# The first norm of a decoder block on one core: rows scaled in place and transposed plainly, the first tokens' products in unsplit fp32, and an earlier place for some weight loads

## The chip, the cores and the metric

One core of a Trainium2 chip runs the whole kernel. The metric is the device time of one launch in microseconds (us); the median of several runs is compared with the median of the kernel before. PE is the matmul engine (TensorE), DVE the vector engine, ACT the scalar engine, POOL is GpSimd, and SP is the engine that issues most loads.

## The reference

```python
# x (512 tokens, 2048), w_in (2048, 3*1024 + 3*1024 + 8 + 2*2048)
h = rmsnorm(x, g_mix)                       # x * rsqrt(mean(x*x) + 1e-6) * g_mix
z = einsum('bsd,dc->bsc', h, w_in)          # all input projections at once
cb, cc, cv, q, k, v, f_logit, gate_c, gate_a = split(z)
conv_y = cb * causal_dwconv(cc * cv, conv_w)
attn = forgetting_attention(q, k, v, log_sigmoid(f_logit + b_f))
merged = sigmoid(gate_c + b1) * (conv_y @ w_conv_out) + sigmoid(gate_a + b2) * (attn @ w_attn_out)
x = x + merged @ w_mix_out
x = x + square(relu(rmsnorm(x, g_mlp) @ w_ff1)) @ w_ff2
out = rmsnorm(x, g_final)
```

All of it is float32. The change lies in the first norm and in the first products with `w_in`.

## The kernel before

**Number format.** A matmul in plain fp32 is avoided in the products. Each operand is cut into a high part, rounded to the reduced format fp32r (`high_of`, ACT, line 111), and the rest, the low part (`low_of`, DVE, line 114). A product is then three matmuls: high by high, low by high, and high by low.

**Tiling.** The 512 tokens are four row tiles of 128 (`xin[0]` to `xin[3]`, 128x2048 each, 1 MB). The 2048 channels are 16 chunks of 128; chunks are taken in pairs, of which the even ones are "parity 0" and the odd ones "parity 1". The products follow a Strassen-like scheme on halves of the tokens and of the channels. For a group of columns the names are A11 and A12 (first half of the tokens, even or odd chunks), A22 (second half of the tokens, odd chunks), and S1 to S4 (sums of halves). `Q1.H[i, par]` holds the normed and transposed tokens of token half i and parity par in fp32; `Q1.ST["A11"]` and so on hold their high and low parts. A group (`Group`) loads its weights in four quarters, `X[i, j]`, 128 x 8 x 256 floats each (1 MB), into four slots. `head` computes the A11 and A12 products, `tail2` the rest. The first group is `gV0`; `heads[1]` is `keys`, the first pair of key and query heads; `heads[2]` to `heads[4]` follow.

**The stage that the change touches** is the first 40 us. Instructions that are `tied` stay in the order in which the program gives them on their engine (`strict[0]`); the others are placed by a scheduler. The order of the kernel before is this:

- SP loads row tile 0 (two halves), `gV0.X[0, 0]` (two pieces), row tile 1 (two halves), `gV0.X[1, 0]`, row tiles 2 and 3, and then the keys' two quarters.
- PE first runs 11 dummy matmuls (`stay_awake`) and transposes the norm's gains (`pv`, line 742).
- ACT and DVE sum the squares of row tile 0 in three pieces. POOL raises the mean to the power -0.5 (`factor`, line 716). DVE multiplies the identity by this factor (line 751, `dgs[0]`), and `Q1.turn` (line 592) multiplies each chunk of rows with this scaled identity, which transposes and scales it at once, in plain fp32. `Q1.gained` (line 600, DVE) takes it out of PSUM and multiplies by the gains.
- `block` (line 697) does the products of one row tile with one weight quarter, kind 0 (high by high), 1 (low rows) and 2 (low weights): 24 matmuls of 256 columns. Tile 0 with A11, then tile 0 with A12, tile 1 with A11, tile 1 with A12, with the turning of tile 1 in between.
- Row tiles 2 and 3 are scaled in place (line 805 on ACT, line 806 on DVE), and `turn_both` and `gained_both` (lines 608, 616, 618) transpose them by plain transposes, 32 in number, through four PSUM banks; DVE takes out four of the eight pairs of chunks and ACT the other four.
- The keys' weights are split (lines 111 and 114), gV0's two sums are added, and A22 is split. Then `g.head()` runs for `heads[1]` and the following groups (`mm_cols`, lines 171, 175 and 177: 48 matmuls of 256 columns a product), then `Q1.sums()`, then the tails, gV0's first (lines 195 to 199).

The high and low parts of weights lie in buffers `th` and `tl`, two of each (`places`).

Of the kernel before, what the change touches and what calls it, by code (L numbers as in the profile page):

```python
# [8 lines left out]
F32 = mybir.dt.float32  # L9
# [36 lines left out]
def tile_hybrid_block(ctx: ExitStack, tc, x, g_mix, w_in, b_f, b_gate, conv_w, w_conv_out,  # L46
# [509 lines left out]
    class Quarters:  # L556
# [134 lines left out]
    def block(n, ps, t, hi, lo, kinds, qs=range(KT // 2)):  # L691

        o, ts = ps[:, t * VW:(t + 1) * VW], slice(t * P, (t + 1) * P)
        for kind in kinds:
            for q in qs:
                Sh, Sl = (e[:, ts] for e in Q1.moving(n)(q))
                tied(nc.tensor.matmul(o, Sl if kind == 1 else Sh, (lo if kind == 2 else hi)[:, q, :],
                                      start=t == 0 and kind == 0 and q == 0, stop=kind == 2 and q == KT // 2 - 1,
                                      skip_group_check=True))

# [23 lines left out]
    nc.vector.memset(ss1[:, :, 4:], EPS)  # L724
    strict[0] = True
    load_rows(0, 2, (nc.sync,))
    gains, rows = both[:KT, 0, S:S + P], both[:NV - KT, 0, S + P:S + 2 * P]
# [28 lines left out]
    tied(nc.gpsimd.dma_start(out=rows[r0:r0 + 3 * CT, :], in_=conv_w[0].rearrange("j (k p) -> (j k) p", p=P)))
    tied(nc.vector.tensor_copy(cols[:, :KT], pv[:, :KT]))
    even, odd = Q1.turn(0, 0, (0, 1)), Q1.turn(0, 1, (2, 5))
    stay_awake(1)
    early, late = range(KT // 4), range(KT // 4, KT // 2)  # L760
    hi1, lo1 = gV0.places()
    for qs in (slice(0, KT // 4), slice(KT // 4, KT // 2)):
        high_of(gV0.X[0, 0][:, qs], hi1[:, qs])
    for n in range(2):
        Q1.gained(0, 0, n, even[n])
    A11, A12 = (Q1.cut(n, 0) for n in ("A11", "A12"))
    high_of(*A11[:2])
    squares(1, 1)
    Q1.gained(0, 1, 0, odd[0])
    low_of(*A11)  # L770
    low_part(gV0.X[0, 0], hi1, lo1, early)
    v = mean_of(1)
    Q1.gained(0, 1, 1, odd[1])
    tied(nc.scalar.activation(out=dgs[1], in_=ident, func=AF.Copy, scale=factor(v)))
    high_of(*A12[:2])
    low_part(gV0.X[0, 0], hi1, lo1, late)
    a, b = (gV0.acc(k)[0] for k in "ab")
    block("A11", a, 0, hi1, lo1, (0, 1))
    block("A11", a, 0, hi1, lo1, (2,), early)
    even = Q1.turn(1, 0, (6, 7))  # L780
    block("A11", a, 0, hi1, lo1, (2,), late)
    odd = Q1.turn(1, 1, (0, 1))
    pv = bank(2, "pv")
    tied(nc.tensor.transpose(pv[:, :NV - KT], rows, ident[:NV - KT, :NV - KT]))
    hi2, lo2 = gV0.places()
    high_of(gV0.X[1, 0], hi2)
    for n in range(2):
        Q1.gained(1, 0, n, even[n])
    low_of(*A12)
    block("A12", b, 0, hi2, lo2, (0, 1))  # L790
    A11, A12 = (Q1.cut(n, 1) for n in ("A11", "A12"))
    high_of(*A11[:2])
    low_of(*A11)
    squares(2, 1)
    squares(3, 1)
    for n in range(2):
        Q1.gained(1, 1, n, odd[n])
    r2 = factor(mean_of(2))
    low_part(gV0.X[1, 0], hi2, lo2, early)
    low_part(gV0.X[1, 0], hi2, lo2, late)  # L800
    r3 = factor(mean_of(3))
    high_of(*A12[:2])
    low_of(*A12)
    tied(nc.scalar.activation(out=cols[:, KT:], in_=pv[:, :NV - KT], func=AF.Copy))
    tied(nc.scalar.activation(out=xin[2], in_=xin[2], func=AF.Copy, scale=r2))
    tied(nc.vector.tensor_scalar(out=xin[3], in0=xin[3], scalar1=r3, scalar2=None, op0=ALU.mult))
    block("A11", a, 1, hi1, lo1, (0, 1, 2))
    block("A12", b, 0, hi2, lo2, (2,))
    block("A12", b, 1, hi2, lo2, (0, 1, 2))
    tied(nc.gpsimd.dma_start(out=bf, in_=b_f.to_broadcast([P, NH])))  # L810
    gV0.a, b = [a], [b]
    keys.ready["A11"] = hi3, lo3 = keys.places()
    high_of(keys.X[0, 0], hi3)
    Q1.tiles("A22")
# [1138 lines left out]
```

## Time and profile before

| | |
|---|---|
| median of 3 runs | 2400.08 us (2398.72 to 2400.45) |
| the profiled execution | 2399.19 us, span of the core 2397.5 us, mean granted clock 0.999 |
| PE busy | 2381.4 us, 99% of the span |
| DVE busy | 2039.6 us, 85% |
| ACT busy | 1235.8 us, 52% |
| POOL busy | 283.0 us, 12% |
| the chain that ended last | PE 91%, DVE 4%, issue 2%, ACT 2%, DMA 1% |

The span is the time from the first to the last instruction of one profiled execution. The run's own time is 1.7 us longer. A plain fp32 matmul leaves two records on PE, the other matmuls leave one.

### The profile page before, as it was taken

To read this page: it belongs to the slowest core of one execution; us is meant where nothing else is said; L and a number is where in the kernel's file an instruction comes from. 1 tells how busy PE (TensorE), PEld (TensorE's weight loads), DVE (VectorE), ACT (ScalarE), POOL (GpSimd) and SP (SyncE) were. 2 spreads that over 40 slices of the span, in tenths; PEclk is the share of its full clock that TensorE was granted. 3 is DMA by queue.
4 is the path that set the end of the run, shared out by engine and by line. 5 is a ranking of instruction groups with operands and counts; after the bars stand their busy time and mean duration, and the time that the engine had idled before them with its cause. 6 is when DMAs were issued, how large, how long until landed. Compare 5 with 4: busy or idle time off the path is not lost.

```text
span 2397.5 us, 41341 instructions
## 1 busy us (share of the span) xinstructions
PE 2381.4 (99%) x17742; PEld 2253.0 (94%) x17742; DVE 2039.6 (85%) x1684; ACT 1235.8 (52%) x1301; POOL 283.0 (12%) x451
## 2 busy tenths in 40 slices
PE   9999999999999999999999999999999999999998
PEld 9999999999999999899999999999998888888886
DVE  8987787888888778889988989888897888889898
ACT  7443656445545534356666666666664333333334
POOL 1100111121111202012200000000001001100000
PEclk9999999999999999999999999999999999999999
DMA  8665544555465756476856465565688557665662
GB/s 279 184 191 154 172 145 151 169 193 173 159 215 175 265 178 223 147 221 223 322 196 232 169 229 198 198 228 198 231 296 302 166 186 254 220 221 183 228 235 98
DMA packets 282199, 491.98 MB, mean 205 GB/s; under 512 B 11676, under 2 KB 191992, under 8 KB 281632
## 3 DMA queue, kind: packets, MB, share of 16 engines
q1 hardware_dynamic: 229280, 277.96, 36.4%
q0 software_dynamic: 49968, 206.39, 23.5%
q10 hardware_dynamic: 2768, 4.99, 0.6%
q8 instruction: 139, 2.28, 0.4%
q14 instruction: 44, 0.36, 0.0%
HBM read 379.70 MB, written 109.07 MB: 204 GB/s over the span
## 4 chain that ended last, share of the span: by engine, by line
PE 91%; DVE 4%; issue 2%; ACT 2%; DMA 1%; POOL 0%; DVEq 0%; POOLq 0%; ACTq 0%; SPq 0%
PE a L171 6%; PE a L175 6%; PE a L177 6%; PE a L199 5%; PE a L195 5%; PE a L197 5%; PE d L171 5%; PE d L175 5%; PE d L177 5%; PE c L177 4%; PE c L171 4%; PE c L175 4%; PE d L197 3%; PE d L195 3%; PE d L199 3%; PE b L171 3%
## 5 line engine op out<-in xcount | busy, mean ns | idle before, releaser
L111 ACT ACTIVATE th<-x 128x2048 fp32r<-128x2048 f32 (+2 forms) x281 | 537.2, 1912 | 454.5 <-DVE x L128 163.0
L114 DVE TENSOR_TENSOR tl<-x,th 128x2048 fp32r<-128x2048 f32 (+2 forms) x282 | 638.9, 2271 | 149.9 <-ACT th L111 144.1
L128 DVE TENSOR_TENSOR x<-x,x 128x2048 f32<-128x2048 f32 (+1 forms) x160 | 365.5, 2285 | 22.1 <-DMA x<-in_w_in_dram 19.4
L111 ACT ACTIVATE th<-y 128x2048 fp32r<-128x2048 f32 (+1 forms) x109 | 185.4, 1702 | 273.4 <-PE a L197 138.7
L114 DVE TENSOR_TENSOR tl<-y,th 128x2048 fp32r<-128x2048 f32 (+1 forms) x109 | 219.2, 2012 | 25.0 <-ACT th L111 24.5
L195 PE MATMUL a<-th,us 128*128 128x512 f32 x508 | 197.7, 389 | 0.0
L197 PE MATMUL a<-th,us 128*128 128x512 f32 x508 | 197.6, 389 | 0.0
L171 PE MATMUL c<-S,th 128*128 128x256 f32 x848 | 195.4, 276 | 0.0
L175 PE MATMUL c<-S,th 128*128 128x256 f32 x848 | 195.1, 276 | 0.0
L171 PE MATMUL a<-S,th 128*128 128x256 f32 x784 | 180.9, 277 | 0.0
L175 PE MATMUL a<-S,th 128*128 128x256 f32 x784 | 180.2, 276 | 0.0
L171 PEld LDWEIGHTS c<-S,th 128*128 128x128 f32 x848 | 159.2, 188 | 0.0
L175 PEld LDWEIGHTS c<-S,th 128*128 128x128 f32 x848 | 159.2, 188 | 0.0
L175 PEld LDWEIGHTS a<-S,th 128*128 128x128 f32 x784 | 147.3, 188 | 0.0
L171 PEld LDWEIGHTS a<-S,th 128*128 128x128 f32 x784 | 147.2, 188 | 0.0
L199 PE MATMUL a<-tl,us 128*128 128x512 f32 x508 | 135.7, 389 | 0.0
L171 PE MATMUL a<-A,th 128*128 128x256 f32 x544 | 125.7, 277 | 0.0
L171 PE MATMUL b<-A,th 128*128 128x256 f32 x544 | 125.5, 276 | 0.0
L171 PE MATMUL d<-S,th 128*128 128x256 f32 x544 | 125.5, 277 | 0.0
L175 PE MATMUL b<-A,th 128*128 128x256 f32 x544 | 125.4, 276 | 0.0
L175 PE MATMUL a<-A,th 128*128 128x256 f32 x544 | 125.4, 276 | 0.0
L171 PE MATMUL d<-A,th 128*128 128x256 f32 x544 | 125.3, 276 | 0.0
(428 smaller groups left out, 6056.9 us busy)
## 6 DMA issues: line engine op xcount, KB each, us to landing
x<-in_w_in_dram SPq DMA_DIRECT2D x85, 1024.0 KB, 5.7
y<-in_w_ff_dram SPq DMA_DIRECT2D x64, 1024.0 KB, 7.4
x<-in_w_ff_dram SPq DMA_DIRECT2D x60, 1024.0 KB, 8.4
us<-s_d POOLq DMA_DIRECT2D x44, 1024.0 KB, 9.0
s_d<-rh POOLq DMA_DIRECT2D x32, 896.0 KB, 5.7
s_d<-r POOLq DMA_DIRECT2D x32, 896.0 KB, 5.8
x<-in_w_mix_out_dram SPq DMA_DIRECT2D x17, 1024.0 KB, 6.7
g_d<-o POOLq DMA_DIRECT2D x32, 256.0 KB, 3.2
```

What stands on the lines that cost most here:

```text
L111: return tied(nc.scalar.activation(out=hi, in_=src, func=AF.Copy))
L114: return tied(nc.vector.tensor_tensor(out=lo, in0=src, in1=hi.bitcast(F32), op=ALU.subtract))
L128: return nc.vector.tensor_tensor(out=out, in0=a, in1=b, op=ALU.subtract)
L171: i = nc.tensor.matmul(o, hi[:, q, js], Sh, start=first and q == 0 and j == 0, stop=False, skip_group_check=True)
L175: nc.tensor.matmul(o, hi[:, q, js], Sl, start=False, stop=False, skip_group_check=True)
L177: i = nc.tensor.matmul(o, lo[:, q, js], Sh, start=False, stop=q == nq - 1, skip_group_check=True)
L195: tied(nc.tensor.matmul(o, Sh, hi[:, q, :], start=begin and q == 0, stop=False, skip_group_check=True))
L197: tied(nc.tensor.matmul(o, Sl, hi[:, q, :], start=False, stop=False, skip_group_check=True))
L199: tied(nc.tensor.matmul(o, Sh, lo[:, q, :], start=False, stop=q == nq - 1, skip_group_check=True))
```

## The change

Row tiles 0 and 1 are scaled in place, the even chunks by DVE and the odd ones by ACT (`scaled`), and are turned by plain transposes. The products of row tile 0 with both weight quarters, and those of row tile 1 with the first half of the first quarter, are made in plain fp32 from `Q1.H` and the loaded weights (`whole_block`); the other products of row tile 1 stay split (`part_block`). For the split ones only the second half of the first weight quarter is cut (`pieces`), in buffers of their own. The squares of row tile 1 are also taken in three pieces; as written, the pieces of row tile 1 begin at columns 0, 512 and 1536, those of row tile 0 at columns 0, 1024 and 1536. The gains are copied out of PSUM by DVE before the last piece of the squares of row tile 0. `gV0.X[1, 0]` is loaded before row tile 1, and the keys' two quarters before row tiles 2 and 3. Row tile 2 is scaled by DVE, not by ACT. The keys' two weight quarters are split within the tied order, and the turning of row tiles 2 and 3 goes between the two products of the keys' head (`between=rest_turned`), with the split of A22 behind it.

```diff
-                    tied(nc.tensor.matmul(pt[:, k, :], xin[t][:, c * P:(c + 1) * P], dgs[t], start=True, stop=True))
+                    tied(nc.tensor.transpose(pt[:, k, :], xin[t][:, c * P:(c + 1) * P], ident))
...
-    dgs = [both[:, 0, t * P:(t + 1) * P] for t in range(2)]
+    early, late = range(KT // 4), range(KT // 4, KT // 2)
+    front, back = slice(0, KT // 4), slice(KT // 4, KT // 2)
...
+    def scaled(t, par, qs, r, vector=True):
+
+        o = xin[t].rearrange("p (q two c) -> p two q c", two=2, c=P)[:, par, qs]
+        if vector:
+            tied(nc.vector.tensor_scalar(out=o, in0=o, scalar1=r, scalar2=None, op0=ALU.mult))
+        else:
+            tied(nc.scalar.activation(out=o, in_=o, func=AF.Copy, scale=r))
+
+    def whole_block(par, ps, t, X, qs):
+
+        o, ts = ps[:, t * VW:(t + 1) * VW], slice(t * P, (t + 1) * P)
+        for q in qs:
+            tied(nc.tensor.matmul(o, Q1.H[0, par][:, q, ts], X[:, q, :], start=t == 0 and q == 0, stop=False,
+                                  skip_group_check=True))
...
+    gV0.ahead(1, 0)
     load_rows(1, 2, (nc.sync,))
-    gV0.ahead(1, 0)
-    load_rows(2, 1, (nc.sync,))
-    load_rows(3, 1, (nc.sync,))
     keys = heads[1]
     keys.ahead(0, 0)
     keys.ahead(1, 0)
+    load_rows(2, 1, (nc.sync,))
+    load_rows(3, 1, (nc.sync,))
     awake, pv = bank(3, "awake"), bank(7, "pv")
     stay_awake(11)
     tied(nc.tensor.transpose(pv[:, :KT], gains, ident[:KT, :KT]))
-    stay_awake(2)
...
+    stay_awake(4)
+
+    squares_by_scalar(0, 0, 0, 1024)
+    squares_by_scalar(0, 1, 1024, 512)
+    tied(nc.vector.tensor_copy(cols[:, :KT], pv[:, :KT]))
+    squares_by_vector(0, 2, 1536, 512)
+    r0 = factor(sum_of(0))
...
+    scaled(0, 0, front, r0)
+    scaled(0, 1, slice(0, KT // 2), r0, False)
+    scaled(0, 0, back, r0)
     even, odd = Q1.turn(0, 0, (0, 1)), Q1.turn(0, 1, (2, 5))
...
+    whole_block(0, a, 0, first, range(KT // 2))
+    for n in range(2):
+        Q1.gained(0, 1, n, odd[n])
+    pieces = [(first[:, q:q + 2], otile([P, 2, VW], "wh", F32R), otile([P, 2, VW], "wl", F32R)) for q in late[::2]]
+    for x2, h2, l2 in pieces:
+        high_of(x2, h2)
...
+    whole_block(1, b, 0, second, range(KT // 2))
+    hi2, lo2 = gV0.places()
+    high_of(second[:, front], hi2[:, front])
+    squares_by_scalar(1, 0, 0, 1024)
+    squares_by_scalar(1, 1, 512, 512)
+    for piece in pieces:
+        low_of(*piece)
+    squares_by_vector(1, 2, 1536, 512)
+    r1 = factor(sum_of(1))
+    high_of(second[:, back], hi2[:, back])
+    low_part(second, hi2, lo2, early)
+    scaled(1, 0, slice(0, KT // 2), r1)
+    scaled(1, 1, slice(0, KT // 2), r1, False)
+    even, odd = Q1.turn(1, 0, (6, 7)), Q1.turn(1, 1, (0, 1))
...
+    keys.ready["A11"] = hi3, lo3 = keys.places()
+    high_of(keys.X[0, 0], hi3)
...
+    whole_block(0, a, 1, first, early)
...
+    part_block("A11", a, of_first, (0, 2, 1), late)
+    part_block("A12", b, of_second, (0, 2), range(KT // 2))
+    low_of(*A12)
+    part_block("A12", b, of_second, (1,), range(KT // 2))
+    low_of(*A11a)
+    low_of(keys.X[0, 0], hi3, lo3)
+    A12 = Q1.cut("A12", 0)
+    high_of(*A12[:2])
...
     squares(2, 1)
     squares(3, 1)
+    keys.ready["A12"] = hi4, lo4 = keys.places()
+    high_of(keys.X[1, 0], hi4)
     r2 = factor(mean_of(2))
+    tied(nc.vector.tensor_scalar(out=xin[2], in0=xin[2], scalar1=r2, scalar2=None, op0=ALU.mult))
+    low_of(*A12)
     r3 = factor(mean_of(3))
-    tied(nc.scalar.activation(out=xin[2], in_=xin[2], func=AF.Copy, scale=r2))
     tied(nc.vector.tensor_scalar(out=xin[3], in0=xin[3], scalar1=r3, scalar2=None, op0=ALU.mult))
+    low_of(keys.X[1, 0], hi4, lo4)
...
-    with tc.issue_after(third.ins):
-        gV0.plus(s1, b)
+    s1 = gV0.snap(gV0.a)
+    gV0.plus(s1, b)
...
+    def rest_turned():
+
+        strict[0] = True
+        Q1.tiles("A22")
+        for n in range(KT // 2):
+            cs = (2 * n, 2 * n + 1)
+            Q1.gained_both(1, cs, Q1.turn_both((2, 3), cs, (6, 7, 2, 5)[n % 4]), n in (0, 1, 3, 6))
+        strict[0] = False
+        Q1.put("A22", Q1.H[1, 1])
+
+    pinned[0] = True
+    keys.head(between=rest_turned)
+    pinned[0] = False
+    for g in heads[2:]:
         g.head()
```

## Rows read from the trace of the kernel before

**Rows 1.** The page: busy us, share of the span, instructions.

```profile
PE 2381.4 (99%) x17742; PEld 2253.0 (94%) x17742; DVE 2039.6 (85%) x1684; ACT 1235.8 (52%) x1301; POOL 283.0 (12%) x451
```

**Rows 2.** Stretches: length; busy PE, PEld, DVE, ACT, POOL; granted clock; DMA share, GB/s.

```profile
0.00:7.00 7.00, 5.42 (x25) 5.17 (x25) 1.31 (x20) 3.24 (x6) 0.88 (x8) 1.00 0.71 229
30.00:65.00 35.00, 35.00 (x310) 34.85 (x309) 34.92 (x23) 23.17 (x22) 2.17 (x3) 1.00 0.72 222
65.00:89.00 24.00, 24.00 (x213) 23.96 (x213) 22.02 (x12) 11.31 (x7) 1.43 (x2) 1.00 0.46 145
```

**Rows 3.** Timeline of DVE and PE: start, us, line, operation, [idle before].

```profile
65.44 2.29 DVE L128 TENSOR_TENSOR x<-x,x 128x2048 f32<-128x2048 f32 x1 [0.48 <-DMA x<-in_w_in_dram]
...
86.06 2.28 DVE L114 TENSOR_TENSOR tl<-x,th 128x2048 fp32r<-128x2048 f32 x1
...
88.41 1.21 PE L199 MATMUL a<-tl,S 128*128 128x256 f32 x8
```

**Rows 4.** Timeline of PE, 0 to 37 us.

```profile
1.57 5.06 PE L684 MATMUL awake<-ident 128*128 128x128 f32 x22 [1.57 <-POOL ident masks.py:199]
6.57 0.28 PE L742 MATMUL pv<-ident,junk 16*128 16x16 f32 x1
...
8.38 3.84 PE L592 MATMUL ptr<-junk,xn 128*128 128x128 f32 x32 [0.88 <-DVE junk L751]
...
28.27 2.35 PE L608 MATMUL ptr<-ident,xn 128*128 128x128 f32 x20
...
35.58 1.98 PE L177 MATMUL a<-A,tl 128*128 128x256 f32 x16
```

**Rows 5.** Timeline of SP's queue: the third, fourth, seventh and eighth megabyte.

```profile
3.59 0.52 SPq L678 DMA_DIRECT2D xn<-in_x_dram  x1
...
4.16 0.45 SPq L237 DMA_DIRECT2D x<-in_w_in_dram  x1
...
8.40 1.12 SPq L237 DMA_DIRECT2D x<-in_w_in_dram  x1
...
9.56 7.14 SPq L237 DMA_DIRECT2D x<-in_w_in_dram  x1
```

**Rows 6.** DMA issues, the same four in order: KB, us from issue to landing.

```profile
xn<-in_x_dram SPq DMA_DIRECT2D x1, 512.0 KB, 8.4
...
x<-in_w_in_dram SPq DMA_DIRECT2D x1, 1024.0 KB, 11.0
...
x<-in_w_in_dram SPq DMA_DIRECT2D x1, 1024.0 KB, 16.3
...
x<-in_w_in_dram SPq DMA_DIRECT2D x1, 1024.0 KB, 18.1
```

**Rows 7.** Timeline of DVE, 6 to 40 us.

```profile
6.40 0.69 DVE L747 CUSTOM_DVE_ANT_0 junk<-xn 128x512 f32<-128x512 f32 x1 [4.72 <-DMA xn<-in_x_dram]
...
8.03 0.29 DVE L751 TENSOR_SCALAR junk<-ident,r 128x128 f32<-128x128 f32 x1 [0.67 <-POOL r L716]
...
9.57 0.69 DVE L600 TENSOR_TENSOR h<-ptr,cols 128x512 f32<-128x512 f32 x1 [0.90 <-PE ptr L592]
...
12.28 1.23 DVE L114 TENSOR_TENSOR A<-h,A 128x1024 fp32r<-128x1024 f32 x1 [0.23 <-ACT A L111]
...
26.03 1.28 DVE L806 TENSOR_SCALAR xn<-xn,r 128x2048 f32<-128x2048 f32 x1
...
28.91 2.44 DVE L616 TENSOR_SCALAR h<-ptr,cols 128x256 f32<-128x256 f32 x6 [1.60 <-PE ptr L608]
...
37.14 2.28 DVE L114 TENSOR_TENSOR A<-h,A 128x2048 fp32r<-128x2048 f32 x1
```

**Rows 8.** Timeline of ACT and of POOL.

```profile
8.02 1.06 ACT L111 ACTIVATE th<-x 128x1024 fp32r<-128x1024 f32 x1 [0.90 <-DMA x<-in_w_in_dram]
...
21.89 1.93 ACT L554 ACTIVATE junk<-xn 128x2048 f32<-128x2048 f32 x1 [0.28 <-DMA xn<-in_x_dram]
...
24.64 0.55 POOL L716 TENSOR_TENSOR r<-v,mhalf 128x1 f32<-128x1 f32 x1 [0.87 <-DVE v L710]
```

More of the change, by code (lines that the diff above doesn't have):

```diff
@@ L689, in low_part @@
         low_of(src[:, qs], hi[:, qs], lo[:, qs])
[L691 to L699, printed above, removed]
     def squares(t, n):
@@ L724, in tile_hybrid_block, with squares_by_vector, squares_by_scalar, sum_of @@
     nc.vector.memset(ss1[:, :, 4:], EPS)
+    early, late = range(KT // 4), range(KT // 4, KT // 2)
+    front, back = slice(0, KT // 4), slice(KT // 4, KT // 2)
+    def squares_by_vector(t, n, c, w):
+        tied(nc.vector.tensor_tensor_reduce(out=junk[:, c:c + w], in0=xin[t][:, c:c + w], in1=xin[t][:, c:c + w],
+                                            scale=1.0 / D, scalar=0.0, op0=ALU.mult, op1=ALU.add,
+                                            accum_out=ss1[:, t, n:n + 1]))
+    def squares_by_scalar(t, n, c, w):
+        tied(square_part(xin[t][:, c:c + w], ss1[:, t, n:n + 1], junk[:, c:c + w]))
+    def sum_of(t):
+        part = stat.tile([P, 1], F32, tag="vf", name="part", bufs=4)
+        tied(nc.vector.tensor_reduce(out=part, in_=ss1[:, t, :], axis=AX.X, op=ALU.add))
+        return part
+    def scaled(t, par, qs, r, vector=True):
[9 more added lines that the diff above has]
+                                  skip_group_check=True))
+    def halves(part, t, qs):
+        return tuple(e[:, qs] for e in Q1.cut(part, t))
     strict[0] = True
     load_rows(0, 2, (nc.sync,))
-    gains, rows = both[:KT, 0, S:S + P], both[:NV - KT, 0, S + P:S + 2 * P]
+    gains, rows = both[:KT, 0, 0:P], both[:NV - KT, 0, P:2 * P]
     tied(nc.scalar.dma_start(out=gains, in_=g_mix[0].rearrange("(k p) -> k p", p=P)))
@@ L767, in tile_hybrid_block @@
+    first, second = gV0.X[0, 0], gV0.X[1, 0]
+    whole_block(0, a, 0, first, range(KT // 2))
[4 more added lines that the diff above has]
+        high_of(x2, h2)
+    A11 = Q1.cut("A11", 0)
     high_of(*A11[:2])
-    squares(1, 1)
-    Q1.gained(0, 1, 0, odd[0])
     low_of(*A11)
-    low_part(gV0.X[0, 0], hi1, lo1, early)
-    v = mean_of(1)
@@ L773, in tile_hybrid_block @@
[L773 to L782, printed above, removed]
+    whole_block(1, b, 0, second, range(KT // 2))
+    hi2, lo2 = gV0.places()
@@ L786, in tile_hybrid_block @@
-    high_of(gV0.X[1, 0], hi2)
+    keys.ready["A11"] = hi3, lo3 = keys.places()
+    high_of(keys.X[0, 0], hi3)
     for n in range(2):
         Q1.gained(1, 0, n, even[n])
-    low_of(*A12)
[L790 to L793, printed above, removed]
+    whole_block(0, a, 1, first, early)
+    A11a, A11b = halves("A11", 1, front), halves("A11", 1, back)
+    high_of(*A11b[:2])
+    high_of(*A11a[:2])
+    Q1.gained(1, 1, 0, odd[0])
@@ new lines, in tile_hybrid_block, with part_block @@
+    low_of(*A11b)
+    Q1.gained(1, 1, 1, odd[1])
+    def part_block(n, ps, weights, kinds, qs):
+        o = ps[:, VW:2 * VW]
+        for kind in kinds:
+            for q in qs:
+                Sh, Sl = (e[:, P:2 * P] for e in Q1.moving(n)(q))
+                tied(nc.tensor.matmul(o, Sl if kind == 1 else Sh, weights(q, kind == 2),
+                                      start=False, stop=kind == kinds[-1] and q == qs[-1], skip_group_check=True))
+    A12 = Q1.cut("A12", 1)
+    high_of(*A12[:2])
@@ L811, in tile_hybrid_block @@
     gV0.a, b = [a], [b]
-    keys.ready["A11"] = hi3, lo3 = keys.places()
-    high_of(keys.X[0, 0], hi3)
-    Q1.tiles("A22")
-    for n in range(KT // 2):
-        cs = (2 * n, 2 * n + 1)
-        last = Q1.gained_both(1, cs, Q1.turn_both((2, 3), cs, (6, 7, 2, 5)[n % 4]), n in (0, 1, 3, 6))
-        if n == 3:
-            third = last
-    low_of(keys.X[0, 0], hi3, lo3)
-    keys.ready["A12"] = hi4, lo4 = keys.places()
-    high_of(keys.X[1, 0], hi4)
-    low_of(keys.X[1, 0], hi4, lo4)
+    s1 = gV0.snap(gV0.a)
```

44 lines of the change are left out of this document (12 added, 32 removed).

## The prediction

> **What bounds the kernel now.** Start with the page's totals: TensorE (PE) is busy for 99% of the span and the vector engine (DVE) for 85% [rows 1]. The reader should see that PE has only 16.1 us without work in the whole program (2397.5 less 2381.4), so there are two ways to save: less PE work, or fewer of those 16 us. The table of stretches comes next [rows 2]: from 30 to 65 us PE is full, and DVE is full too (34.92 of 35 us); from 65 to 89 DVE idles for only 2 us. So right behind the part that is changed there are two full engines, and what either is late there is not made up. The rows at 88 us show how near they run [rows 3]: DVE ends a low part at 86.06 + 2.28 = 88.34, and the PE matmul that reads it starts at 88.41. A time won on PE alone before that point is lost there, but for 0.07 us, if DVE doesn't come sooner as well. Between 30 and 88 us the only spare time of DVE that doesn't hang on its own work is one wait of 0.48 us for a load.
>
> **The start.** Today the first row tile's factor makes a scaled identity (DVE, 8.03), and PE begins at 8.38 [rows 4, 7]. Sixteen fp32 matmuls leave 32 PE records, two each; (3.84 - 0.28) / 31 = 0.115 us a record. A transpose leaves one record at the same pace (20 in 2.35 us). So 32 matmuls turned into transposes (two row tiles) save 32 records, 3.6 us of PE. Against it, the copy of the gains now stands on DVE ahead of the squares of the first tile. The copy reads pv, which PE ends at 6.57 + 0.28 = 6.85 [rows 4]; squares that start at 6.40 today start at about 7.05, and the factor comes 0.65 later, at 8.68. Then 512 elements a partition are scaled in place: between a quarter of the 2048-wide scaling, 0.32, and the 512-wide PSUM read, 0.69 [rows 7]; I take 0.45, since it is SBUF to SBUF as the former, with a fixed part. First transpose 9.2, 0.8 later than today. ScalarE (ACT) scales the odd chunks meanwhile (1.06, done by 9.85 [rows 8]), so the transposes run through to 11.0. DVE's four gain multiplications (0.69 each) end at 11.2 for the even and 12.4 for the odd chunks. The first products start at 11.0, against 12.2 today (8.38 + 3.84).
>
> **The unsplit products.** Twenty matmuls of 256 columns in plain fp32 take the place of sixty split ones, which cost 0.113 each ((1.98 - 0.28) / 15 [rows 4]), 6.8 us. No row has a plain fp32 matmul of 256 columns. Lower bound of a record: 0.113, as for 256 columns split; upper: twice the 128-column record, 0.227. I take the upper, as the row with the same data type is the nearer. Then the twenty cost 9.1 (40 x 0.227), 2.3 more than now; at the lower bound 4.5, 2.3 less. The Trainium skill (FP8 and Floating Point Precision, section TensorE Precision Notes) says that true fp32 makes four passes through the array, which speaks against trading three split products for one. Estimated from that at 2.4 GHz, one takes 0.43 us and twenty take 8.5, and the result below would not move; no row shows it at 256 columns. By the upper bound the first two blocks (8 matmuls, 3.63 each) end at 14.6 and 18.26.
>
> **Second row tile.** Loads arrive in the order in which they are issued. Today the third, fourth, seventh and eighth megabyte land at 3.59 + 8.4 = 12.0, 15.2, 24.7 and 27.7 [rows 5, 6]. The change puts the second weight quarter third and the second row tile fourth, the keys fifth and sixth, rows 2 and 3 seventh and eighth. So the second row tile is complete at 15.2 instead of 12.0. Its factor: DVE squares 0.69, the sum, and 0.8 for POOL's power with its wait (0.55 + some 0.25 [rows 8]), 16.9. DVE first does a low part that stands ahead (1.23), then scales 1024 elements (half of 1.28 up to 1.23; I take 0.74): 18.1. PE comes at 18.26, so no wait. With the cheap fp32 PE would come at 14.6 and wait until 18.2: the price that I can't see changes nothing. Sixteen transposes (1.8), the transposed parameters, four fp32 matmuls (1.8) and twelve split ones (1.4) bring PE to 23.35. The next block needs ACT's high part, which follows four gain steps of DVE (19.0 to 22.3) and takes 1.06: 23.5. Its 24 matmuls end at 26.3. Today this point is 28.27, where the joint transposes of rows 2 and 3 begin [rows 4]. So far 2.0 us are won.
>
> **Where they go.** Now the keys' first product (48 x 0.113 = 5.44) comes before those transposes, and ends at 31.7. The transposes need rows 2 and 3 scaled, both on DVE (today one was on ACT). DVE: low parts until 27.6 (the last, 2.28, for the keys); row 2 landed at 24.7 and its squares take 1.93 + 0.2 on ACT, so its sum is taken at 27.6, POOL's power holds DVE until 28.35, scaling to 29.6 (1.28), a low part to 30.8; only then the sum of row 3, whose squares were done at 29.8; power 31.7, scaling 33.0. PE starts the transposes at 33.1: 1.4 us idle. Behind the scaling DVE has the keys' second low part (2.28, to 35.15) in its queue ahead of the evacuations of the transposes. There are four PSUM banks; the fifth group of transposes waits for the first evacuation (2 x 0.41), 36.05, and so on; they end at 38.15 instead of 35.3 without waits. The keys' second product ends at 43.6; today that is 35.58 + 1.81 + 5.44 = 42.83. PE is 0.8 us late, the whole gain gone. DVE: four pairs of evacuations and the low part of A22 end at about 40.8, with a gap of some 0.4 for the seventh group, against 37.14 + 2.28 = 39.4 [rows 7]: 1.3 to 1.7 late, of which the load's 0.48 at 65 us is taken up [rows 3]. At 88.4 us both ask for +0.8 to +1.2. I take +0.9. Costed at nothing: ACT's extra high parts, hidden by its free time (11.8 of 35 us from 30 to 65 [rows 2]); the keys' weights sooner, since their high and low parts are ready by 27.6, behind which PE reads the low part only at 29.9 (if they were late, each us would be one of PE); the first head's sums, in DVE's wait for POOL at 27.6.
>
> The sum is made against the profiled execution (2399.19 us, span 2397.5): 2399.19 + 0.9 = 2400.1, which is the median of the runs (2400.08). I forecast no change.
>
> **Rivals.** *The 2 us come through (faster).* If rows 2 and 3 are scaled in time and the keys' low part doesn't hold the evacuations, PE ends the keys at 40.8; if in addition DVE's order until 88 us is such that the matmul at 88.4 isn't held, the time is 2399.2 - 2.0 = 2397.2. For it: PE has less work by 3.6 - 2.3 = 1.3 us and starts 1.2 sooner. Against: DVE has no spare time there [rows 2, 3]. It decides if the first joint transpose starts before 32 us and no gap follows.
>
> *The PE clock falls (slower).* The first 22 records run at 5.06 / 22 = 0.23 us [rows 4], twice the 0.115 of the full level, 2.4 GHz, so at the pace of the lower one, 1.2 GHz, although the granted clock reads 1.00 there [rows 2]. The change puts idle time and transposes one after the other in two places: 7.9 to 11.0 and 31.7 to 38.15. If PE falls to half pace in one of them for as long as at the start, 5.06 us, it does 2.5 us of work less: 0.9 + 2.5 gives 2402.6; in both, 2405.1. It decides if the first product after a stretch of transposes runs at twice 0.113. Against: after the 32 joint transposes of today the matmuls run at 0.113 at once. The Trainium skill (TensorE: Matmul & The Clock Gate, section Part 4: PE-mode transpose) says that the full clock does not engage for transposes; by that both stretches would be followed by slow matmuls, and the time would be the 2405.1; the trace of today doesn't bear it out.
>
> *The loads don't come in the new order's places (slower).* PE waits for row 3, so each us that it lands after 27.7 is one us. To be slower by 0.2% it would have to land 4.9 us later, at 32.6. For: one issue on this queue took 7.14 us [rows 5]. Against: nothing is added to the queue ahead of it.
>
> **How the numbers follow.** Forecast 0.54 (2398.3 to 2401.8); 2 us come through 0.22; clock 0.10; late loads 0.06; the scheduler orders the rest of the program otherwise, either way, 0.08. A measurement of this kernel tells about 0.2%, 4.8 us, from no change. Faster by more: 0.03 of the second case and 0.05 of the last, 0.08. Slower by more: 0.03 of the clock's, 0.04 of the loads', 0.03 of the last, 0.10. The rest, 0.82, is the same. Range 2396.6 (second case with the runs' scatter of 0.6 below) to 2403.4 (one fall of the clock and 0.8).
>
> **What would show it.** Right: first transposes near 9.2, products from 11.0 with records 0.227 apart, the joint transposes idle at 31.7 to 33.1 and again behind the fourth group, DVE's A22 low part 1 to 2 us later, the head's end 0.5 to 1 us later than 42.83. Wrong: fp32 records at 0.113 with a wait at 14.6 (a wrong price with the same end); no wait at the joint transposes; a half-speed pace after them; or a gap of PE beyond 44 us that today's kernel doesn't have.

## The result, and the profile after

The changed kernel takes 2404.87 us (median of 17 runs, 2402.58 to 2406.86) beside 2400.14 us for the kernel before (17 runs): a ratio of 1.0019, 95% interval [1.0012, 1.0027]. It is slower by 4.7 us, at the edge of what the prediction called no change (4.8 us), and outside its range (2396.6 to 2403.4). Unaltered and run once more it took 2403.99 us, ratio 1.0013 [1.0004, 1.0023], beside 2400.53 us for the kernel before in the same series: 3.5 us.

The page's totals of the changed kernel answer to [rows 1]: PE has 50 records fewer and is busy 3.1 us longer, in a span 5.9 us longer.

```profile
PE 2384.5 (99%) x17692; PEld 2253.8 (94%) x17692; DVE 2042.1 (85%) x1690; ACT 1234.7 (51%) x1305; POOL 284.5 (12%) x451
```

The timeline of PE in the changed kernel, 8 to 45 us, beside [rows 4]:

```profile
9.15 1.97 PE L592 MATMUL ptr<-ident,xn 128*128 128x128 f32 x16 [0.92 <-DVE xn L737]
10.96 3.62 PE L745 MATMUL a<-x,h 128*128 128x256 f32 x16
14.42 3.62 PE L745 MATMUL b<-x,h 128*128 128x256 f32 x16
18.76 1.96 PE L592 MATMUL ptr<-ident,xn 128*128 128x128 f32 x16 [0.73 <-DVE xn L737]
...
26.75 0.28 PE L171 MATMUL a<-A,th 128*128 128x256 f32 x1
...
30.51 2.05 PE L177 MATMUL a<-A,tl 128*128 128x256 f32 x16
32.40 0.27 PE L608 MATMUL ptr<-ident,xn 128*128 128x128 f32 x1
33.14 1.85 PE L608 MATMUL ptr<-ident,xn 128*128 128x128 f32 x15 [0.47 <-DVE xn L864]
...
36.22 0.63 PE L608 MATMUL ptr<-ident,xn 128*128 128x128 f32 x4 [0.16 <-DVE h L616]
...
37.05 1.47 PE L608 MATMUL ptr<-ident,xn 128*128 128x128 f32 x12
...
42.13 2.05 PE L177 MATMUL b<-A,tl 128*128 128x256 f32 x16
```

Up to here PE does nearly what was forecast: transposes at 9.15 (9.2), products at 10.96 (11.0) with records (14.42 - 10.96) / 16 = 0.216 apart (0.227), the joint transposes at 33.14 (33.1) with a second stop behind the fourth group, the head's end at 44.0 (43.6). PE idles only 0.47 ahead of the joint transposes, not 1.4, because the keys' first product begins at 26.75 (26.3) and its matmuls come (30.51 - 26.75) / 32 = 0.1175 apart, not 0.113. The larger difference is on DVE. Its timeline in the changed kernel, beside [rows 7], and ACT's:

```profile
25.62 2.28 DVE L114 TENSOR_TENSOR tl<-x,th 128x2048 fp32r<-128x2048 f32 x1
...
31.80 1.28 DVE L864 TENSOR_SCALAR xn<-xn,r 128x2048 f32<-128x2048 f32 x1 [0.69 <-POOL r L706]
33.00 2.28 DVE L114 TENSOR_TENSOR tl<-x,th 128x2048 fp32r<-128x2048 f32 x1
35.20 2.44 DVE L616 TENSOR_SCALAR h<-ptr,cols 128x256 f32<-128x256 f32 x6
37.56 2.28 DVE L114 TENSOR_TENSOR tl<-x,th 128x2048 fp32r<-128x2048 f32 x1
39.76 0.87 DVE L616 TENSOR_SCALAR h<-ptr,cols 128x256 f32<-128x256 f32 x2
42.66 2.29 DVE L114 TENSOR_TENSOR A<-h,A 128x2048 fp32r<-128x2048 f32 x1 [2.03 <-ACT A L111]
```

```profile
36.88 2.52 ACT L618 ACTIVATE h<-ptr,cols 128x256 f32<-128x256 f32 x6 [1.45 <-PE ptr L608]
40.71 1.92 ACT L111 ACTIVATE A<-h 128x2048 fp32r<-128x2048 f32 x1 [1.31 <-issue]
```

The same place in the kernel before, DVE and then ACT:

```profile
31.86 0.86 DVE L616 TENSOR_SCALAR h<-ptr,cols 128x256 f32<-128x256 f32 x2
32.65 4.57 DVE L114 TENSOR_TENSOR tl<-x,th 128x2048 fp32r<-128x2048 f32 x2
...
39.34 2.28 DVE L114 TENSOR_TENSOR tl<-x,th 128x2048 fp32r<-128x2048 f32 x1
```

```profile
34.79 1.91 ACT L111 ACTIVATE A<-h 128x2048 fp32r<-128x2048 f32 x1
```

The reader should follow one dependence. A22's low part (DVE, line 114) needs A22's high part (ACT, 1.9 us), and that needs the last evacuation of the joint transposes. Before, DVE had two low parts to do behind its last evacuation (32.65 to 37.14), the keys' first and second, and they covered ACT's high part (34.79 to 36.70). In the changed kernel both stand ahead of the evacuations (25.62 and 33.00). A third low part, that of the next group's first quarter, came behind A22's in the kernel before (39.34); it is not tied, and the scheduler has put it into the gap before the last pair (37.56). So the last pair comes at 39.76, ACT's high part starts at 40.71, and DVE, with nothing left to do, waits from 40.63 to 42.66.

Two stretches sum it up: from DVE's first gain multiplication to the point from which these three low parts are still to do, and from there until they and A22's are done; the kernel before and then the changed one (length; busy PE, PEld, DVE, ACT, POOL; granted clock; DMA share, GB/s).

```profile
9.57:24.89 15.32, 14.82 (x126) 14.22 (x125) 13.54 (x18) 13.01 (x15) 2.69 (x5) 1.00 1.06 376
24.89:41.62 16.73, 16.73 (x150) 16.59 (x149) 15.13 (x16) 13.81 (x17) 1.59 (x3) 1.00 0.80 246
```

```profile
9.85:25.62 15.77, 15.04 (x96) 13.55 (x95) 13.63 (x20) 12.58 (x17) 1.90 (x2) 1.00 1.06 379
25.62:44.95 19.33, 18.70 (x160) 18.29 (x159) 16.55 (x20) 15.06 (x18) 3.75 (x4) 1.00 0.88 277
```

DVE is 44.95 - 41.62 = 3.33 us behind: 0.28 from the start, 13.63 + 16.55 - 13.54 - 15.13 = 1.51 of more work, and the rest, 1.54, of more idle time, nearly all of it the 2.03. From there to 88 us [rows 3] its work is the same, in another order, and the low part that PE reads at 88.41 in the kernel before comes 3.25 later. The timeline of the changed kernel, DVE and PE:

```profile
89.31 2.29 DVE L114 TENSOR_TENSOR tl<-x,th 128x2048 fp32r<-128x2048 f32 x1
...
91.66 0.62 PE L199 MATMUL a<-tl,S 128*128 128x256 f32 x3 [0.34 <-DVE tl L114]
```

### The profile page after: what moved, and what is told of

It reads as the page before. It is cut to its first block, busy times and chain, and to the rows that moved or that the text cites. A ratio compares the mean times of both kernels' runs of the same rounds, so it can differ in the third digit from the quotient of the medians.

```text
span 2403.4 us, 41261 instructions
## 1 busy us (share of the span) xinstructions
PE 2384.5 (99%) x17692; PEld 2253.8 (94%) x17692; DVE 2042.1 (85%) x1690; ACT 1234.7 (51%) x1305; POOL 284.5 (12%) x451
## 4 chain that ended last, share of the span: by engine, by line
PE 87%; DVE 6%; issue 3%; ACT 2%; DMA 1%; POOL 1%; SPq 0%; DVEq 0%; POOLq 0%; ACTq 0%
PE a L171 6%; PE a L177 6%; PE a L175 6%; PE d L171 5%; PE a L199 5%; PE d L175 5%; PE d L177 5%; PE a L197 5%; PE a L195 5%; PE c L177 4%; PE c L171 4%; PE c L175 4%; PE d L195 3%; PE d L197 3%; PE d L199 3%
```

## The experiments

All kernels are compared by five numbers. The median time, and its ratio to the kernel before as measured in the same series (2399.92 to 2400.53 us). How far DVE is behind the kernel before when it has ended the sum h<-h,h, the sum for o and the low part that stand behind A22's low part (46.62 us there). How far PE is behind at its only line-164 matmul c<-S,th (103.59 us there) and at the first matmul of line 193 on M (999.33 us there).

| kernel | time, us | ratio [95% interval] | DVE at 46.6 | PE at 103.6 | PE at 999.3 |
|---|---|---|---|---|---|
| before_copy | 2402.33 | one run | +0.3 | -0.2 | +0.1 |
| before_plus | 2402.94 | 1.0009 [1.0001, 1.0018] | +2.3 | +1.7 | +2.0 |
| the changed kernel | 2404.87 | 1.0019 [1.0012, 1.0027] | +3.3 | +2.7 | +3.9 |
| after_again | 2403.99 | 1.0013 [1.0004, 1.0023] | +3.2 | +2.6 | +3.6 |
| low4_behind | 2403.51 | 1.0012 [1.0004, 1.0021] | +2.7 | +1.7 | +3.0 |
| evac_by_act | 2404.11 | 1.0013 [1.0004, 1.0021] | +2.8 | +1.8 | +3.2 |
| norm_alone | 2409.75 | 1.0034 [1.0021, 1.0047] | +7.2 | +7.9 | +8.7 |
| row2_by_act | 2404.77 | 1.0019 [1.0010, 1.0028] | +3.0 | +2.5 | +4.1 |
| rows_first | 2403.36 | 1.0013 [1.0004, 1.0022] | +2.5 | +1.5 | +2.3 |
| rows_first_act | 2404.39 | 1.0018 [1.0009, 1.0027] | +2.8 | +2.9 | +3.7 |
| rows_first_zero | 2405.29 | 1.0022 [1.0012, 1.0033] | +3.8 | +3.2 | +4.1 |
| rows_first_turned | 2402.96 | 1.0013 [1.0004, 1.0022] | +2.4 | +1.4 | +2.7 |
| row3_unscaled | 2402.32 | 1.0009 [0.9999, 1.0019] | +1.8 | +1.2 | +2.0 |
| factor_sooner | 2402.65 | 1.0010 [1.0001, 1.0020] | +2.2 | +1.2 | +2.1 |
| rows_first_more_pe | 2433.24 | one run | - | - | - |

Three theories were set against each other at first: A, DVE is behind at 45 us and hands it to PE at 82 to 92 us; B, a slower pace of PE, which the trace of the changed kernel showed up to 92 us; C, a loss near 1020 to 1170 us that has nothing to do with the first norm.

**after_again**: the changed kernel, unaltered.

> The changed kernel unaltered, for a second trace. Theory A (the vector engine falls 3.3 us behind, waiting for the split of A22, and hands this to PE at 82 to 92 us) expects the same places again: DVE idle for some 2.0 us ahead of the low part of A22, PE waits at the start of S3 and of S2, PE 2.7 to 3.3 us later than the kernel before at 104 us. Theory B (PE's matmuls come 0.1176 us apart instead of 0.1134 from 27 to 92 us, and this is the loss) expects the slower pace again in that stretch. Theory C (2 us of the loss arise between 1020 and 1170 us and have nothing to do with the first stage) expects them to come and go from trace to trace; A and B expect nothing there. Time 2404 to 2406 by all three.

Two stretches of the changed kernel, then the same of after_again:

```profile
40.00:50.00 10.00, 10.00 (x87) 10.00 (x86) 7.97 (x7) 6.21 (x4) 0.72 (x1) 1.00 0.54 158
50.00:60.00 10.00, 10.00 (x87) 10.00 (x86) 10.00 (x6) 5.91 (x4) 0.73 (x1) 1.00 0.82 252
```

```profile
40.00:50.00 10.00, 10.00 (x91) 10.00 (x90) 7.96 (x7) 6.14 (x4) 0.72 (x1) 1.00 0.52 158
50.00:60.00 10.00, 10.00 (x90) 10.00 (x90) 10.00 (x6) 6.49 (x4) 0.73 (x1) 1.00 0.84 252
```

One program ran at 87 matmuls in 10 us and at 90 to 91, with PE full and the granted clock at 1.00 both times, and PE is at the same place at 104 us (+2.7 and +2.6). B falls: PE's place at 104 us does not follow its pace.

**low4_behind** and **evac_by_act** each go at DVE's wait of 2.03.

```diff
-    low_of(keys.X[1, 0], hi4, lo4)
...
             Q1.gained_both(1, cs, Q1.turn_both((2, 3), cs, (6, 7, 2, 5)[n % 4]), n in (0, 1, 3, 6))
+        low_of(keys.X[1, 0], hi4, lo4)
```

> The changed kernel with the keys' second low part placed behind the evacuations of the joint transposes instead of ahead of them. Theory A: the last evacuation ends some 2 us sooner, ACT's high part of A22 too, DVE's 2.0 us wait ahead of A22's low part goes, so PE's waits at 82 to 92 us shrink from 1.8 to under 0.5; 1.5 to 2.5 us faster than the changed kernel, about 2402.5 to 2403.4. Theory B: the pace is the same, so within 0.7 us of the changed kernel. Theory C: within 1 us of it at most.

```diff
-            Q1.gained_both(1, cs, Q1.turn_both((2, 3), cs, (6, 7, 2, 5)[n % 4]), n in (0, 1, 3, 6))
+            Q1.gained_both(1, cs, Q1.turn_both((2, 3), cs, (6, 7, 2, 5)[n % 4]), n in (0, 1, 3))
```

> The changed kernel with one pair of evacuations (the seventh of eight) given from DVE to ACT. Theory A: DVE has 0.8 us less work and the high part of A22 no longer waits for a DVE evacuation that stands behind another low part; DVE's idle time of 2.0 us falls to under 1 and the time by 1 to 2 us, to 2403 to 2404. Theory B: no change (under 0.7 us). Theory C: no change.

DVE's timeline in low4_behind:

```profile
31.97 1.29 DVE L864 TENSOR_SCALAR xn<-xn,r 128x2048 f32<-128x2048 f32 x1 [0.68 <-POOL r L706]
33.90 2.44 DVE L616 TENSOR_SCALAR h<-ptr,cols 128x256 f32<-128x256 f32 x6 [0.64 <-PE ptr L608]
36.81 0.88 DVE L616 TENSOR_SCALAR h<-ptr,cols 128x256 f32<-128x256 f32 x2 [0.47 <-PE ptr L608]
37.60 4.48 DVE L114 TENSOR_TENSOR tl<-x,th 128x2048 fp32r<-128x2048 f32 x2
42.01 2.28 DVE L114 TENSOR_TENSOR A<-h,A 128x2048 fp32r<-128x2048 f32 x1
```

Two low parts (the keys' second and the next group's first) cover ACT's high part again, and the 2.03 is gone. But without a low part ahead of the evacuations DVE waits 0.64 and 0.47 for PE's transposes, so that it gains 0.7 and PE 1.0 at 104 us, where A had expected 1.5 to 2.5 in the time; the time is 0.5 less than that of after_again, and the intervals overlap. In evac_by_act the wait stays at 2.12, since ACT does the last pair and the high part one after the other; DVE gains 0.5 by its smaller work. Both times the result is below the expectation: neither move alone mends the order of three engines in these 10 us.

**norm_alone**: the new first norm, with the old order of the loads, and the keys' splits and the joint transposes where they stand in the kernel before, ahead of the keys.

```diff
+    load_rows(1, 2, (nc.sync,))
     gV0.ahead(1, 0)
-    load_rows(1, 2, (nc.sync,))
-    keys = heads[1]
-    keys.ahead(0, 0)
-    keys.ahead(1, 0)
     load_rows(2, 1, (nc.sync,))
     load_rows(3, 1, (nc.sync,))
+    keys = heads[1]
+    keys.ahead(0, 0)
+    keys.ahead(1, 0)
...
-    keys.head(between=rest_turned)
```

> The first part of the change alone: rows 0 and 1 scaled in place, plain transposes and unsplit fp32 products stay; the loads stand in the old order, and the joint transposes and the split of the keys' weights in their old place ahead of the keys' products. Theory A: the vector engine has no wait for row 3 and none for A22, so the gain that PE has at 26 us (2.0 us in the changed kernel's plan) is lost at most to DVE's extra 1 to 2 us of work; 2398.5 to 2401. Theory B: it depends on the pace: about 2400 if PE keeps 0.1134 from 27 to 88 us, 2402 or more if not. Theory C: 2 us over what A says, 2400.5 to 2403, if the loss between 1020 and 1170 us shows in this one too.

No theory had this in it (2409.75 us). Without the keys' first product there is nothing between the second row tile and the joint transposes, and PE stands almost still. Stretches of norm_alone, and its joint transposes on PE:

```profile
28.00:34.00 6.00, 1.90 (x14) 1.33 (x12) 4.52 (x6) 4.82 (x6) 2.50 (x3) 1.00 0.76 249
34.00:36.00 2.00, 2.00 (x10) 2.00 (x11) 1.15 (x3) 0.00 (x0) 0.78 (x2) 0.52 0.40 109
36.00:38.00 2.00, 2.00 (x13) 2.00 (x12) 1.17 (x4) 0.86 (x3) 0.00 (x0) 0.63 0.06 25
```

```profile
33.98 3.96 PE L608 MATMUL ptr<-ident,xn 128*128 128x128 f32 x19 [0.37 <-DVE xn L859]
...
37.90 1.48 PE L608 MATMUL ptr<-ident,xn 128*128 128x128 f32 x12
```

PE has 1.90 us of work in 6, and then the granted clock is 0.52 and 0.63, near the lower level of 1.2 GHz, for the first 19 joint transposes; it is 1.00 again from 38 us, and the other twelve run at (1.48 - 0.28) / 11 = 0.109 each. So the other parts of the change, the loads and the keys' splits and product moved forward, belong to the new first norm: together they don't bring time, they cover what it leaves open. The run undoes them all at once and doesn't say which counts.

**before_plus** tests A on the kernel before, where nothing else is different.

```diff
     low_of(keys.X[1, 0], hi4, lo4)
+    low_of(keys.X[1, 0], hi4, lo4)
```

> The kernel before, with one more low part of the keys' second quarter on VectorE (2.28 us, the same values written twice, the result unchanged) at about 38 us. Theory A (VectorE has no spare time before 88 us, so that what it falls behind in the first 45 us is given to TensorE whole): the low part that TensorE waits for at 88.3 us comes 2.0 to 2.3 us later, the waits of TensorE at 82 to 92 us grow by as much, and the time is 2402.0 to 2403.5 us. The rival (VectorE's lag is covered by TensorE's own lead and the changed kernel's loss comes from elsewhere, its TensorE above all): under 0.5 us at 104 us, and a time within 1 us of the kernel before.

The timeline of before_plus, DVE and PE, beside [rows 3]:

```profile
87.79 2.28 DVE L114 TENSOR_TENSOR tl<-x,th 128x2048 fp32r<-128x2048 f32 x1
...
90.13 1.20 PE L199 MATMUL a<-tl,S 128*128 128x256 f32 x8 [0.39 <-DVE tl L114]
```

2.28 us of work for DVE alone, at about 38 us, and PE reads the low part at 90.13, 1.72 later; 2.0 are left at 999 us, and the time is 0.09% more. A holds, less a quarter (it had the low part 2.0 to 2.3 later): of a delay of DVE in this stretch only about 0.5 us is taken up, the size of the one wait for a load [rows 3], which is gone here, and the rest is in the time.

**row2_by_act, rows_first, rows_first_act** build on low4_behind. The first has the first edit of these, the keys' second high part moved behind it, the second the other edit, the third both.

```diff
-    tied(nc.vector.tensor_scalar(out=xin[2], in0=xin[2], scalar1=r2, scalar2=None, op0=ALU.mult))
+    tied(nc.scalar.activation(out=xin[2], in_=xin[2], func=AF.Copy, scale=r2))
...
-    keys.ahead(1, 0)
     load_rows(2, 1, (nc.sync,))
     load_rows(3, 1, (nc.sync,))
+    keys.ahead(1, 0)
```

> The changed kernel with the keys' second low part behind the evacuations, and row 2 scaled by ScalarE in place of VectorE (1.28 us less work of VectorE), the keys' second high part behind it on ScalarE. Theory A (VectorE's work before 45 us sets the time): about 1 us less than with the low part moved alone, 2402.0 to 2402.8 us, and at 104 us some 0.7 us behind the kernel before, not 1.7. The rival (VectorE waits there for TensorE's transposes, which wait for row 3, and less work only makes it wait longer): no difference, 2403.3 to 2403.8 us.

> The changed kernel with the keys' second low part behind the evacuations, and with rows 2 and 3 loaded ahead of the keys' second weight quarter. Theory A, in its sharper form (row 3 comes late and the evacuations behind it are what idles VectorE): row 3 is scaled by about 31 us in place of 33.3, VectorE has no idle time of over 0.3 us from 30 to 44 us, the transposes go as one group, and the time falls by 1.5 to 2.5 us against the low part moved alone, to 2401.0 to 2402.0 us. The rival (the amount of VectorE's work is the limit, whatever its order): under 0.7 us better, 2402.8 us or more.

> Both edits together: rows 2 and 3 loaded ahead of the keys' second quarter, the keys' second low part behind the evacuations, and row 2 scaled by ScalarE. Theory A: VectorE loses neither the work nor the idle time, and is at 45 us where it was in the kernel before or up to 0.6 us ahead; the time is 2399.5 to 2401.0 us, no more than the kernel before. The rival (something after 104 us costs the changed kernel 1 to 2 us, whatever its first part does): 2401.5 us or more although the traces stand level at 104 us.

Row 2 on ACT was a loss: row 3 is scaled 0.5 sooner (31.43), although DVE waits 1.64 for POOL's factor, but ACT's evacuations start 0.8 later (35.56 against 34.77), DVE then waits 1.33 for PE, and at 104 us the kernel is 0.8 behind low4_behind. A missed its sign; the rival had the longer wait right, but had expected no difference. The keys' second high part was moved as well, so that the loss is not that of the scaling alone. rows_first_act has the same two waits. With 2404.39 us and +2.9 at 104 us it meets neither side: A had 2399.5 to 2401.0 us, and its rival, whose 2401.5 us or more it reaches, had the traces level at 104 us. Rows 2 and 3 loaded sooner gave 0.2, not 1.5 to 2.5: row 3 was scaled at 31.79, hardly sooner than 31.97. A's sharper form, that the loading of row 3 makes DVE late, falls. In these kernels row 3's factor is asked of DVE behind the scaling of row 2 and a low part, whenever the row landed.

**row3_unscaled** and **factor_sooner** go at that, the one in the changed kernel, the other in rows_first.

```diff
-    tied(nc.vector.tensor_scalar(out=xin[3], in0=xin[3], scalar1=r3, scalar2=None, op0=ALU.mult))
...
+    r3 = factor(mean_of(3))
     low_of(*A12)
-    r3 = factor(mean_of(3))
```

> The changed kernel with row 3 left unscaled: its scaling (1.29 us of VectorE) and the wait for its factor (0.69 us) are left out of the computation. Theory A (what VectorE is behind at 45 us is handed to TensorE whole): VectorE comes to 45 us some 2.0 us sooner, the milestone at 104 us stands 0.5 to 1.0 us behind the kernel before in place of 2.7, and the time is 2401.5 to 2403.0 us. The rival (TensorE's transposes and ScalarE's split of the evacuated block are what VectorE waits for, so that less work of its own only lengthens its wait): under 0.7 us at 104 us, 2403.8 us or more.

> The kernel with rows 2 and 3 loaded first and the keys' second low part behind the evacuations, with the mean of row 3 asked of VectorE ahead of a low part of 1.22 us, so that GpSimd works out its factor meanwhile. Theory A: the 0.69 us in which VectorE waits for GpSimd goes, row 3 is scaled at about 31.1 us in place of 31.8, and 104 us comes 0.5 to 0.8 us sooner, some 0.8 us behind the kernel before; the time 2402.5 to 2403.0 us, less than the changed kernel and more than the kernel before. The rival (VectorE then waits as much longer for TensorE's transposes): under 0.2 us.

With 1.28 us of work and the wait of 0.69 left out, DVE is 1.6 sooner than in the changed kernel and PE 1.5 at 104 us (+1.2 against +2.7); at 999 us it is 1.8, and the time 2402.32 us stands where A put it (its 104 us does not: 0.5 to 1.0 was expected). The wait for A22's high part is the same (2.04), so it was DVE's work and its wait for the factor that counted. factor_sooner cut POOL's wait only to 0.46 and brought 0.3: in the expected direction, half the size, and its time (2402.65 us) does not differ from that of rows_first by more than the intervals.

**rows_first_zero** was meant as the counterpart of before_plus and failed as a test.

```diff
-        low_of(keys.X[1, 0], hi4, lo4)
...
     r3 = factor(mean_of(3))
+    tied(nc.gpsimd.memset(lo4.bitcast(F32), 0.0))
```

> The kernel with rows 2 and 3 loaded first and the keys' second low part behind the evacuations, with that low part not computed by VectorE (2.28 us) but set to zero by GpSimd, idle at that time: the low products of this quarter are left out of the result, TensorE's work is the same. Theory A (the amount of VectorE's work before 45 us is handed to TensorE at 82 to 92 us): 1.7 to 2.3 us less than the same kernel with the low part, thus 2401.0 to 2401.7 us, level with the kernel before at 104 us, within 0.7. The rival (the joint transposes and ScalarE's splits hold the row of work up, VectorE only waits longer): under 0.7 us at 104 us.

Timeline of POOL and DVE in rows_first_zero:

```profile
31.60 1.80 POOL L864 MEMSET tl<- 128x2048 f32 x1
...
31.67 2.80 DVE L865 TENSOR_SCALAR xn<-xn,r 128x2048 f32<-128x2048 f32 x1 [0.69 <-POOL r L706]
```

Beside the memset DVE's scaling took 2.80 us in place of 1.29, and with the low part gone from behind the evacuations the wait for A22's high part was back (2.38). It tells nothing against A; row3_unscaled was run in its place.

**before_copy, rows_first_turned, rows_first_more_pe** ask about theory C: after 999 us the first two profiles drew apart by 2 us more. The two others change, in rows_first, which buffers later tiles fall on (the first edit) and how many instructions PE has had by then (the second).

> The kernel before, unaltered, profiled a second time. Two things are read from it: how far the milestones of one program vary from one profile to the next (theory D: by up to 1 us in all, so that the 5 to 6 us between the two profiled spans overstate a difference of 4), and whether TensorE waits near 1080 us for ScalarE's split, which waits for a transfer of staged to h_d. Theory E (the changed first norm alters how these transfers run) expects no such wait, the transfer issued at about 1065 us landing in 6.7 to 7.1 us; the rival, chance from profile to profile, expects it to come up in one unaltered program as in the other.

```diff
+    otile([P, 2, VW], "spare")
+    gV0.places()
...
-    stay_awake(4)
+    for i in range(84):
+        tied(nc.tensor.matmul(awake[:, :8], ident, ident[:, :8], start=True, stop=True))
```

> The kernel with rows 2 and 3 loaded first, with one more pair of split buffers and one more small buffer taken in the first norm and not used, so that every later tile falls on the same one of the rotating buffers as in the kernel before. Theory E1 (the growth near 1080 us comes from where the buffers lie): the wait of TensorE for ScalarE there, 1.1 to 1.9 us in the profiles of the changed kernel, goes, the transfer of staged to h_d issued at 1064 to 1069 us lands in 6.7 to 7.1 us in place of 7.8 to 8.7, and the span at 1183 us grows by no more than 0.7 us over that at 999 us against the kernel before. Its rivals (the instruction count, or chance): nothing changes there, 2403.0 to 2404.0 us.

> The kernel with rows 2 and 3 loaded first, with the last four matmuls that keep TensorE's clock up replaced by 84 of 8 columns, so that TensorE's instructions after them have nearly the same numbers as in the kernel before. The start of the first transposes comes up to 4 us later. Theory E2 (the growth near 1080 us comes from where in its program an engine fetches instructions, which shifts with the count): the wait near 1080 us goes and the transfer to h_d lands in 6.7 to 7.1 us. Its rivals (buffers, or chance): the wait of 1 to 2 us stays, only later by what the start costs.

ACT in the kernel before (the profile of the rows), and then ACT and PE in before_copy, the same program:

```profile
1072.08 0.63 ACT L111 ACTIVATE staged<-f 128x512 fp32r<-128x512 f32 x1 [5.56 <-DMA h_d<-staged]
```

```profile
1074.04 0.63 ACT L111 ACTIVATE staged<-f 128x512 fp32r<-128x512 f32 x1 [7.47 <-DMA h_d<-staged]
...
1077.04 0.39 PE L195 MATMUL d<-th,M 128*128 128x256 f32 x1 [1.81 <-ACT th L111]
```

before_copy is level with the first profile at 999 us (+0.1), and 3.1 us behind it at the end (span 2400.6), more than the 1 us that theory D allowed: a transfer out lands 1.9 us later, and PE waits 1.81 for the split that stands behind it; where the other 1.2 arises was not followed. So the wait near 1080 us comes and goes in one unaltered program, and theory E, that it takes the changed first norm to slow these transfers, falls. That the change has no part in it is not shown: one of the three profiles with the old first norm has the wait (before_plus has none), and all twelve of the changed kernel and its variants that start in time have it, 0.53 to 1.94 us long. In rows_first_turned it was 0.6 us, which after this proves nothing for the buffers; rows_first_more_pe started 30 us late, not the 4 us expected (below), and can't be used.

## Why the prediction was wrong, point by point

**Right.** What bounds the stretch: DVE, with about half a microsecond to spare, and PE behind it. before_plus shows it by itself. The loads landed in the forecast order, and the start, row 3's scaling (31.80, forecast 31.7) and the joint transposes were within 0.2 us; PE's gain before them was 1.5 (26.75 against 28.27), not 2.0, because the second row tile's transposes came at 18.76, 0.5 late behind its factor, and all of it was lost at the joint transposes, as forecast. The unseen price of plain fp32 was near the upper bound and changed nothing. The faster rival's condition, joint transposes before 32 us, was not met, and the loads kept their places. PE's clock did not fall after the transposes of the changed kernel: the granted clock is 1.00 in its stretches above. So the clock rival's price for two falls, 2405.1, lies beside the measured time by chance. The Trainium skill (TensorE: Matmul & The Clock Gate, section Part 4: PE-mode transpose) says that the full clock does not engage for transposes; in this kernel 16 of them in a row run at (1.97 - 0.28) / 15 = 0.113 us each at a granted clock of 1.00, and 16 in rows_first_more_pe at (3.65 - 0.28) / 15 = 0.225 at 0.50, so the measurement decides against it here. In norm_alone the clock even came back to 1.00 behind a row of 19 transposes (above).

**The step that failed** is the one about DVE behind the transposes: "four pairs of evacuations and the low part of A22 end at about 40.8, with a gap of some 0.4 for the seventh group", DVE "1.3 to 1.7 late". A22's low part started 5.5 us late (42.66 against 37.14), because the next group's first low part now stands ahead of it; with that one counted on both sides DVE was 3.33 late. The work was sized about right (1.51 more, and 0.28 from the start); the idle time was 2.03 and not 0.4. I had counted DVE's own instructions and the transposes that feed them, and not what stands between the last evacuation and A22's low part on ACT, a high part of 1.92. The keys' second low part was costed as an instruction moved ahead of the evacuations; that it had been the cover for ACT's high part was left out. And the gap for the seventh group did not stay empty: the low part of 2.28 that the scheduler put there (37.56) held back the last pair, and ACT stands idle for 1.31 ahead of its high part. low4_behind, where both low parts stand behind the evacuations, has no such wait; it moves the two together, and no run tells which of them counts for more. The prediction had "the scheduler orders the rest of the program otherwise" only as a chance of 0.08, without a mechanism.

**The hand-over.** I let the load's 0.48 be taken up and came to +0.9 at 88 us. With 3.33 in place of 1.3 to 1.7 it is 3.25 at 88 us and 2.7 at 104 us: the wait for the load is gone, but a wait of DVE for a high part of ACT, 1.47 at 79.20 in the kernel before, is 2.06 at 82.45. before_plus (2.3 to 1.7) and row3_unscaled (1.6 less gives 1.5 less) hand over 0.75 and 0.95 of theirs, the changed kernel 0.81.

**After 104 us.** The changed kernel is another 1.2 behind at 999 us (after_again 1.0), and all its variants 0.8 to 1.7, the two with the old first norm 0.2 and 0.3. In the changed kernel 0.7 of it is a second wait at one line, which all twelve profiles of kernels with the new first norm that start in time have and the three with the old one don't; PE's waits from 104 to 440 us, kernel before and changed kernel (us in total, times, longest):

```profile
PE tp L982 <- ACT p L974: 0.6, 1, 0.6
```

```profile
PE tp L1038 <- ACT p L1030: 1.3, 2, 0.7
```

What makes it come twice stays open, and so does the rest.

**The base.** The sum was made against a profiled execution of 2399.19 us. before_copy shows that this one was without a wait of 1.8 us that another execution of the same program has; the median of the runs was 0.9 above it. So the forecast of +0.9 came out as "no change" only because it was added to an execution 0.9 below the median. From the median, 2400.1 + 2.7 + 1.2 = 2404.0, an estimate from single profiles, near the two measurements of the changed kernel (2404.87 and 2403.99).

None of the versions is faster than the kernel before; the interval of row3_unscaled alone, which leaves work out, reaches 1.0. The change leaves PE 50 records fewer, though not less busy time by the page, and gives DVE 1.51 us more to do in a stretch where DVE is already full [rows 2].

## What to carry to other kernels

Where an engine is full for 50 us behind a change, most of a microsecond added on it can end up in the time (here 0.75 to 0.95 of it reached PE), whatever the fullest engine of the page wins; test it by doubling one of its instructions in the kernel before. When an instruction is moved, ask what it covered at its old place: here low parts of 2.28 us on DVE had hidden a high part of 1.92 us on ACT. Look also at what the scheduler puts into a gap that the change leaves. And take a second profile of the unaltered kernel before explaining a difference far from the change.

## What the runs showed of the hardware

**A clock that falls while PE is busy.** In rows_first_more_pe 84 matmuls of 8 columns in plain fp32, two records each, took 32.90 us. Its PE timeline and two stretches:

```profile
6.78 32.90 PE L771 MATMUL awake<-ident 128*128 128x8 f32 x168
```

```profile
10.00:20.00 10.00, 10.00 (x50) 10.00 (x49) 0.00 (x0) 0.85 (x2) 0.26 (x1) 0.51 1.07 382
20.00:30.00 10.00, 10.00 (x49) 10.00 (x48) 0.00 (x0) 0.00 (x0) 0.00 (x0) 0.50 0.54 194
```

PE counts as busy throughout, and the granted clock is 0.50, the level of 1.2 GHz, from 10 to 40 us (30 to 40 reads as the two shown); a record of 8 columns takes 0.196, beside 0.23 for one of 128 columns at the start [rows 4].

**POOL beside DVE.** A memset by POOL more than doubled a scaling on DVE that ran at the same time, 1.29 to 2.80 us (rows_first_zero). The Trainium skill (GPSIMD Engine Reference, section Specifications) has the two engines share their interfaces to SBUF, with contention for some forms of DVE instructions; the trace agrees in so far, with this number, and no run shows whether this scaling is one of those forms.

**Two paces of PE** at a granted clock of 1.00: 87 and 90 to 91 matmuls of 256 columns in 10 us, in the same stretch of two executions of one program. No run shows what chooses between them.
